# Rotary embedding on one core: four slots for x, and GpSimd products over eight positions

## The chip, the core and the metric

The kernel runs on one of the eight NeuronCores of a Trainium2 chip. A core has five engines that run their own instruction streams: TensorE (PE; its weight loads are shown apart as PEld), VectorE (DVE), ScalarE (ACT), GpSimd (POOL) and SyncE (SP). They work on SBUF, an on-chip memory of 128 partitions, and PSUM, a smaller one that TensorE writes and that GpSimd does not use here. Sixteen DMA engines move data between SBUF and the chip's main memory (HBM); transfers are issued from a queue of SP (q1 in the profile) or of ACT (q10).

The metric is the device time of one launch in microseconds (us), the median of several runs. Next to it stands one profiled execution, from which all rows are taken.

## The reference

x has the shape 8 x 2048 x 8 x 64 in float32 (batch, position, head, width): 33.55 MB in, and as much out. cos and sin are 2048 x 32.

```python
def reference(x, cos, sin):
    x1 = x[..., : x.shape[-1] // 2]
    x2 = x[..., x.shape[-1] // 2 :]
    cos = cos[None, :, None, :]
    sin = sin[None, :, None, :]
    out1 = x1 * cos - x2 * sin
    out2 = x1 * sin + x2 * cos
    return np.concatenate([out1, out2], axis=-1)
```

So every element of the output is one product with cos and one product with sin of the other half of its head, added.

## The kernel before

**Tiling.** A batch is spread over the 128 partitions with 16 positions on each; a position has 8 x 64 = 512 elements (HD), so a partition holds 8192 elements, 32 KB, of a batch. A batch is worked off in pieces, mostly of four positions (UNIT, 2048 elements); the first and the last batch have some pieces of two (lines 170 to 175).

**Buffers.** x lies in a pool of NBUF slots of 32 KB (line 45). The result overwrites x in its slot and is stored from there, so a slot is free for another batch only when the batch's stores have landed. The sin products lie in a pool `t2p` of three buffers (line 46), the cos products in one PSUM tile (`t1p`) or in a pool of two SBUF tiles (`t1s`).

**A piece** (`rotate`, line 102) is of one of three kinds:

- A, the usual one: GpSimd makes the two sin products of the halves (line 122: two instructions, each over half of the elements, one with sin and one with -sin) into a `t2` tile; VectorE makes the cos product (line 129) into PSUM and adds the two into x (line 136).
- B, the first piece of batches 2, 4 and 5: the products as in A, but the cos product goes to SBUF, and TensorE adds the two with identity matrices into PSUM (lines 143 and 144), from where ScalarE copies the sum into x (line 145).
- C, the first piece of batches 1 and 3: VectorE makes both products (lines 129 and 148), TensorE adds (lines 160 and 161), ScalarE copies (line 165). GpSimd has nothing to do.

**Order.** Each engine runs its instructions in the order of the program: `keep` holds them to it. The loop at the end goes over the batches, and in each over the pieces. Loads are issued by SP: the first NBUF batches ahead of the loop (the first batch in three parts, with the tables cos and sin after the first of them), and batch b + NBUF at the end of batch b (line 193), where it waits for b's stores. Stores are issued by ACT, one for each whole batch; the first batch is stored in three parts, and the last batch in three parts by SP (line 74).

Of the kernel before, what the change touches and what calls it, by code (L numbers as in the profile page):

```python
# [9 lines left out]
@with_exitstack  # L10
def kernel(
    ctx: ExitStack,
    tc: tile.TileContext,
    x: bass.AP,
    cos: bass.AP,
    sin: bass.AP,
    out: bass.AP,
):
    nc = tc.nc
    keep = tc.keep_in_program_order  # L20
    f32 = mybir.dt.float32
    PSUM = bass.MemoryType.PSUM

    B, S, H, D = x.shape
    Dh = D // 2
    P = 128
    HD = H * D
    R = S // P
    ROW = R * HD
    UNIT = 4 * HD  # L30
    NBUF = 5
    C = 512
    last = B - 1

    xv = x.rearrange("b (q r) h d -> b q (r h d)", q=P)
    ov = out.rearrange("b (q r) h d -> b q (r h d)", q=P)
    cos_src = cos.rearrange("(q r) d -> q r d", q=P)
    sin_src = sin.rearrange("(q r) d -> q r d", q=P)

    const_pool = ctx.enter_context(tc.tile_pool(name="const", bufs=1))  # L40
    tab_pool = ctx.enter_context(tc.tile_pool(name="tab", bufs=1, space=PSUM))
    t1_pool = ctx.enter_context(tc.tile_pool(name="t1p", bufs=1, space=PSUM))
    o_pool = ctx.enter_context(tc.tile_pool(name="op", bufs=1, space=PSUM))
    t1s_pool = ctx.enter_context(tc.tile_pool(name="t1s", bufs=2))
    xpool = ctx.enter_context(tc.tile_pool(name="xpool", bufs=NBUF))
    t2_pool = ctx.enter_context(tc.tile_pool(name="t2p", bufs=3))

    cos_sb = const_pool.tile([P, R, Dh], f32, tag="cb")
    sin_sb = const_pool.tile([P, R, Dh], f32, tag="sb")
    nsin = const_pool.tile([P, R, Dh], f32, tag="ns")  # L50
    eye = const_pool.tile([P, P], f32, tag="eye")
    neye = const_pool.tile([P, P], f32, tag="neye")
    cos_ps = tab_pool.tile([P, R, Dh], f32, tag="cp")
    sin_ps = tab_pool.tile([P, R, Dh], f32, tag="sp")

    xts = {}

    def spans(sizes):
        lo = 0
        for n in sizes:  # L60
            yield lo, n
            lo += n

    def load(b):
        xt = xpool.tile([P, ROW], f32, tag="xt", name=f"xt{b}")
        for lo, n in spans([UNIT, UNIT, 2 * UNIT] if b == 0 else [ROW]):
            keep(nc.sync.dma_start(out=xt[:, lo : lo + n], in_=xv[b, :, lo : lo + n]))  # L67
            if b == 0 and lo == 0:
                keep(nc.sync.dma_start(out=cos_sb, in_=cos_src))  # L69
                keep(nc.sync.dma_start(out=sin_sb, in_=sin_src))  # L70
        xts[b] = xt

    def store(b, lo, n):
        queue = nc.sync if b == last else nc.scalar
        keep(queue.dma_start(out=ov[b, :, lo : lo + n], in_=xts[b][:, lo : lo + n]))  # L75

    for b in range(NBUF):
        load(b)

    nc.gpsimd.memset(eye, 0.0)  # L80
    nc.gpsimd.affine_select(
        out=eye,
        in_=eye,
        compare_op=mybir.AluOpType.not_equal,
        fill=1.0,
        base=0,
        pattern=[[-1, P]],
        channel_multiplier=1,
    )
    keep(nc.scalar.mul(nsin, sin_sb, -1.0))  # L90
    keep(nc.scalar.copy(sin_ps, sin_sb))  # L91
    keep(nc.scalar.mul(neye, eye, -1.0))
    keep(nc.vector.tensor_copy(cos_ps, cos_sb))  # L93

    def rep(a, n):
        return dataclasses.replace(a, ap=[a.ap[0][:], a.ap[1][:], [0, n], a.ap[-1][:]])

    kinds = {}
    for b, kind in ((1, "C"), (2, "B"), (3, "C"), (4, "B"), (5, "B")):
        kinds[(b, 0)] = kind  # L100

    def rotate(b, lo, n):
        kind = kinds.get((b, lo), "A")
        xt = xts[b][:, lo : lo + n]
        r0 = lo // HD
        nr = n // HD
        xk = xt.rearrange("p (r k d) -> p r k d", r=nr, d=Dh)
        xu = xt.rearrange("p (g u d) -> p g u d", u=2, d=Dh)
        if kind == "A":
            t1 = t1_pool.tile([P, n], f32, tag="t1")  # L110
        else:
            t1 = t1s_pool.tile([P, n], f32, tag="t1s")
        if kind == "C":
            t2 = t1s_pool.tile([P, n], f32, tag="t1s")
        else:
            t2 = t2_pool.tile([P, n], f32, tag="t2")
        t1u = t1.rearrange("p (g u d) -> p g u d", u=2, d=Dh)
        t2u = t2.rearrange("p (g u d) -> p g u d", u=2, d=Dh)
        if kind != "C":
            for u, tab in ((1, sin_sb), (0, nsin)):  # L120
                keep(
                    nc.gpsimd.tensor_mul(  # L122
                        out=t2u[:, :, u, :].rearrange("p (r h) d -> p r h d", h=H),
                        in0=xu[:, :, 1 - u, :].rearrange("p (r h) d -> p r h d", h=H),
                        in1=rep(tab[:, r0 : r0 + nr, :], H),
                    )
                )
        keep(
            nc.vector.tensor_mul(  # L129
                out=t1.rearrange("p (r k d) -> p r k d", r=nr, d=Dh),  # L130
                in0=xk,
                in1=rep(cos_ps[:, r0 : r0 + nr, :], 2 * H),
            )
        )
        if kind == "A":
            keep(nc.vector.tensor_add(out=xt, in0=t1, in1=t2))  # L136
        elif kind == "B":
            for j in range(n // (2 * C)):
                o = o_pool.tile([P, 2 * C], f32, tag="o")
                for k in range(2):  # L140
                    cs = slice((2 * j + k) * C, (2 * j + k + 1) * C)
                    oc = o[:, k * C : (k + 1) * C]
                    nc.tensor.matmul(oc, eye, t1[:, cs], start=True, stop=False)  # L143
                    nc.tensor.matmul(oc, eye, t2[:, cs], start=False, stop=True)  # L144
                keep(nc.scalar.copy(xt[:, 2 * j * C : 2 * (j + 1) * C], o))  # L145
        else:
            keep(
                nc.vector.tensor_mul(  # L148
                    out=t2.rearrange("p (r k d) -> p r k d", r=nr, d=Dh),
                    in0=xk,  # L150
                    in1=rep(sin_ps[:, r0 : r0 + nr, :], 2 * H),
                )
            )
            G = C // Dh
            for u in range(2):
                o = o_pool.tile([P, n // 2], f32, tag="o")
                for j in range(n // 2 // C):
                    oc = o[:, j * C : (j + 1) * C]
                    gs = slice(j * G, (j + 1) * G)
                    nc.tensor.matmul(oc, eye, t1u[:, gs, u, :], start=True, stop=False)  # L160
                    nc.tensor.matmul(  # L161
                        oc, eye if u else neye, t2u[:, gs, 1 - u, :], start=False, stop=True
                    )
                keep(
                    nc.scalar.copy(  # L165
                        xu[:, :, u, :], o.rearrange("p (g d) -> p g d", d=Dh)
                    )
                )

    def pieces(b):  # L170
        if b == 0:
            return [2 * HD, 2 * HD, UNIT, UNIT, UNIT]
        if b == last:
            return [UNIT, UNIT, UNIT, 2 * HD, 2 * HD]
        return [UNIT] * 4

    def shares(b):
        if b == 0:
            return [HD, 7 * HD, 2 * UNIT]
        if b == last:  # L180
            return [2 * UNIT, UNIT, UNIT]
        return [ROW]

    for b in range(B):
        done = 0
        outs = list(spans(shares(b)))
        for lo, n in spans(pieces(b)):
            rotate(b, lo, n)
            done = lo + n
            while outs and sum(outs[0]) <= done:  # L190
                store(b, *outs.pop(0))
        if b + NBUF <= last:
            load(b + NBUF)

# [29 lines left out]
```

## Time and profile before

| | before |
|---|---|
| median of 3 runs | 163.81 us (163.28 to 164.0) |
| span of the profiled execution | 161.6 us |
| data moved by DMA | 67.65 MB, a mean of 419 GB/s over the span |
| VectorE, last add ends | 153.4 us |
| last store issued | 153.4 us, landed 7.3 us later |
| 4 MB loads of x, issue to landing | median 39.0 us |
| 4 MB stores, issue to landing | median 28.3 us |

The page of a profile gives for each engine the busy time, its share of the span and the number of instructions; then the span in 40 equal slices with a digit for the busy share of each slice in tenths (9 is 90% or more), for the DMA engines too. The groups of instructions name line, engine, operation, output and inputs with their shapes, the number of instructions; then the busy time and the mean duration in ns; then the idle time of the engine just ahead of them with what ended it. The order of time has the start in us, the duration in us, the engine, the line, and in brackets the idle time of the engine ahead of it with its releaser. The DMA view of a stretch gives the packets and bytes that each queue moved in it, and their share of the 16 engines' time. Releasers and waits are inferred by the profiler from semaphores.

### The profile page before, as it was taken

The page shows a single profiled execution, that of the slowest core. Times are in us where ns is not written, and L with a number is a line of the kernel's source. Part 1 is how long each engine was busy: PE and PEld are TensorE (multiplying, and loading weights), DVE is VectorE, ACT ScalarE, POOL GpSimd, SP SyncE. Part 2 cuts the span into 40 slices and gives each one's busy share as a digit, 9 for nine tenths or more (in the row PEclk, how much of TensorE's full clock was granted, in tenths as well). Part 3 has the DMA queues.
Part 4 walks back from the last instruction along what each step waited for, and adds up shares of the span by engine and source line. Part 5 has one row for each costly group of instructions (what it writes and reads, how often), then busy time and mean ns, then how long its engine had stood idle before and what let it go on. Part 6 is the DMA issues. An engine that isn't in the chain of part 4 may idle for free.

```text
span 161.6 us, 460 instructions
## 1 busy us (share of the span) xinstructions
PE 47.2 (29%) x80; PEld 17.8 (11%) x80; DVE 140.1 (87%) x66; ACT 12.8 (8%) x14; POOL 139.0 (86%) x70
## 2 busy tenths in 40 slices
PE   0000000497208760878029752972000000000000
PEld 0000000133003210222014211330000000000000
DVE  0468899999999999999999999999899998999900
ACT  3200000002200220021000220022000000000000
POOL 1299999999999899999996999998999969999200
PEclk9999999999965997599855998799555555555555
DMA  5999998899999999999999999999999999999995
GB/s 183 414 442 467 424 472 373 373 430 503 398 389 454 454 454 389 471 438 389 471 438 389 454 456 389 446 454 398 446 448 406 446 446 406 446 446 430 385 414 215
DMA packets 3458, 67.65 MB, mean 419 GB/s; under 512 B 384, under 2 KB 384, under 8 KB 768
## 3 DMA queue, kind: packets, MB, share of 16 engines
q1 hardware_dynamic: 2160, 38.27, 55.8%
q10 hardware_dynamic: 1296, 29.36, 42.2%
q14 instruction: 2, 0.02, 0.0%
HBM read 34.08 MB, written 33.55 MB: 419 GB/s over the span
## 4 chain that ended last, share of the span: by engine, by line
DMA 46%; DVE 37%; POOL 9%; issue 2%; SPq 1%; DVEq 0%; POOLq 0%; ACTq 0%
DMA xt<-in_x_dram 24%; DVE t L129 18%; DMA out_dram<-xt 18%; DVE xt L136 17%; POOL t L122 9%; DMA sin_sb<-in_sin_dram 3%; DVE t L148 1%; SPq L69 0%; SPq L67 0%; DVEq L136 0%; POOLq L122 0%; ACTq L75 0%
## 5 line engine op out<-in xcount | busy, mean ns | idle before, releaser
L122 POOL TENSOR_TENSOR t<-xt,sin_sb 128x1024 f32<-128x1024 f32 (+1 forms) x32 | 70.5, 2204 | 10.8 <-DMA sin_sb<-in_sin_dram 5.8
L129 DVE TENSOR_TENSOR t<-xt,cos_ps 128x2048 f32<-128x2048 f32 (+1 forms) x34 | 73.4, 2166 | 0.8
L122 POOL TENSOR_TENSOR t<-xt,nsin 128x1024 f32<-128x1024 f32 (+1 forms) x32 | 70.5, 2203 | 0.0
L136 DVE TENSOR_TENSOR xt<-t,t 128x2048 f32<-128x2048 f32 (+1 forms) x29 | 62.2, 2144 | 6.1 <-POOL t L122 3.7
L143 PE MATMUL o<-t,eye 128*128 128x512 f32 x24 | 16.5, 778 | 23.7 <-DVE t L129 20.2
L160 PE MATMUL o<-t,eye 128*128 128x512 f32 x16 | 10.6, 749 | 39.1 <-DVE t L129 36.9
L144 PE MATMUL o<-t,eye 128*128 128x512 f32 x24 | 14.7, 701 | 0.0
L145 ACT COPY xt<-o 128x1024 f32<-128x1024 f32 x6 | 6.1, 1012 | 45.7 <-PE o L144 45.7
L143 PEld LDWEIGHTS o<-t,eye 128*128 128x128 f32 x24 | 5.3, 244 | 32.8 <-issue 26.8
L160 PEld LDWEIGHTS o<-t,eye 128*128 128x128 f32 x16 | 3.6, 247 | 44.5 <-POOL t L122 30.6
L165 ACT COPY xt<-o 128x1024 f32<-128x1024 f32 x4 | 4.0, 1012 | 47.1 <-PE o L161 47.1
L144 PEld LDWEIGHTS o<-t,eye 128*128 128x128 f32 x24 | 5.7, 239 | 8.0 <-issue 8.0
L93 DVE COPY cos_ps<-cos_sb 128x512 f32<-128x512 f32 x1 | 0.7, 695 | 6.3 <-DMA cos_sb<-in_cos_dram 6.3
L161 PE MATMUL o<-t,neye 128*128 128x512 f32 x8 | 6.0, 847 | 0.2 <-DVE t L148 0.2
L148 DVE TENSOR_TENSOR t<-xt,sin_ps 128x2048 f32<-128x2048 f32 x2 | 4.6, 2279 | 0.0
L161 PE MATMUL o<-t,eye 128*128 128x512 f32 x8 | 4.1, 592 | 0.0
L161 PEld LDWEIGHTS o<-t,neye 128*128 128x128 f32 x8 | 1.8, 251 | 4.3 <-issue 2.7
L161 PEld LDWEIGHTS o<-t,eye 128*128 128x128 f32 x8 | 1.5, 190 | 1.9 <-issue 1.9
L90 ACT ACT_TABLE_LOAD x1 | 1.3, 1283 | 0.7 <-PEq L208 0.7
L90 ACT ACTIVATE nsin<-sin_sb 128x512 f32<-128x512 f32 x1 | 0.6, 630 | 5.0 <-DMA sin_sb<-in_sin_dram 5.0
L91 ACT COPY sin_ps<-sin_sb 128x512 f32<-128x512 f32 x1 | 0.6, 579 | 0.0
L80 POOL MEMSET eye<- 128x128 f32 x1 | 0.2, 205 | 0.3 <-POOLq L208 0.3
(6 smaller groups left out, 1.0 us busy)
## 6 DMA issues: line engine op xcount, KB each, us to landing
xt<-in_x_dram SPq DMA_DIRECT2D x7, 4096.0 KB, 39.0
out_dram<-xt ACTq DMA_DIRECT2D x6, 4096.0 KB, 28.3
xt<-in_x_dram SPq DMA_DIRECT2D x2, 1024.0 KB, 6.1
xt<-in_x_dram SPq DMA_DIRECT2D x1, 2048.0 KB, 11.5
out_dram<-xt ACTq DMA_DIRECT2D x1, 2048.0 KB, 25.3
out_dram<-xt SPq DMA_DIRECT2D x1, 2048.0 KB, 12.3
out_dram<-xt SPq DMA_DIRECT2D x2, 1024.0 KB, 8.7
out_dram<-xt ACTq DMA_DIRECT2D x1, 1792.0 KB, 20.2
```

The lines of the kernel that those rows point to most:

```text
L90: keep(nc.scalar.mul(nsin, sin_sb, -1.0))
L93: keep(nc.vector.tensor_copy(cos_ps, cos_sb))
L122: nc.gpsimd.tensor_mul(out=t2u[:, :, u, :].rearrange("p (r h) d -> p r h d", h=H), in0=xu[:, :, 1 - u, :].rearrange("p (r h) d -> p r h d" ...
L129: nc.vector.tensor_mul(out=t1.rearrange("p (r k d) -> p r k d", r=nr, d=Dh), in0=xk, in1=rep(cos_ps[:, r0 : r0 + nr, :], 2 * H),)
L136: keep(nc.vector.tensor_add(out=xt, in0=t1, in1=t2))
L143: nc.tensor.matmul(oc, eye, t1[:, cs], start=True, stop=False)
L144: nc.tensor.matmul(oc, eye, t2[:, cs], start=False, stop=True)
L145: keep(nc.scalar.copy(xt[:, 2 * j * C : 2 * (j + 1) * C], o))
L148: nc.vector.tensor_mul(out=t2.rearrange("p (r k d) -> p r k d", r=nr, d=Dh), in0=xk, in1=rep(sin_ps[:, r0 : r0 + nr, :], 2 * H),)
L160: nc.tensor.matmul(oc, eye, t1u[:, gs, u, :], start=True, stop=False)
L161: nc.tensor.matmul(oc, eye if u else neye, t2u[:, gs, 1 - u, :], start=False, stop=True)
L165: nc.scalar.copy(xu[:, :, u, :], o.rearrange("p (g d) -> p g d", d=Dh))
```

## The change

The number of slots for x goes from five to four. The sin products are taken out of `rotate` into a new function `cross`, which makes them for a span of its own, named by a new function `wides`. In batch 0 the spans are 2, 2, 4 and 8 positions; in batches 1 and 3, whose first piece needs none, 4 and 8; in batches 2 and 4, 8 and 8; in batches 5 and 6, 4, 4 and 8; in batch 7 they are the pieces themselves, as before. `rotate` takes the part that it needs out of the wide tile. The pool `t2p` still has three buffers, which are now of 16 KB instead of 8 KB on each partition. The pieces, kinds, cos products, adds and stores stay as they are.

```diff
-    NBUF = 5
+    NBUF = 4
...
+    t2s = {}
+
+    def cross(b, lo, n):
+        xt = xts[b][:, lo : lo + n]
+        r0 = lo // HD
+        nr = n // HD
+        xu = xt.rearrange("p (g u d) -> p g u d", u=2, d=Dh)
+        t2 = t2_pool.tile([P, n], f32, tag="t2")
+        t2u = t2.rearrange("p (g u d) -> p g u d", u=2, d=Dh)
+        for u, tab in ((1, sin_sb), (0, nsin)):
+            keep(
+                nc.gpsimd.tensor_mul(
+                    out=t2u[:, :, u, :].rearrange("p (r h) d -> p r h d", h=H),
+                    in0=xu[:, :, 1 - u, :].rearrange("p (r h) d -> p r h d", h=H),
+                    in1=rep(tab[:, r0 : r0 + nr, :], H),
+                )
+            )
+        t2s[b] = (t2, lo, n)
+
     def rotate(b, lo, n):
...
         if kind == "C":
             t2 = t1s_pool.tile([P, n], f32, tag="t1s")
         else:
-            t2 = t2_pool.tile([P, n], f32, tag="t2")
+            wide, wlo, wn = t2s[b]
+            t2 = wide[:, lo - wlo : lo - wlo + n]
         t1u = t1.rearrange("p (g u d) -> p g u d", u=2, d=Dh)
         t2u = t2.rearrange("p (g u d) -> p g u d", u=2, d=Dh)
-        if kind != "C":
-            for u, tab in ((1, sin_sb), (0, nsin)):
-                keep(
-                    nc.gpsimd.tensor_mul(
...
-                    )
-                )
...
+    def wides(b):
+        if b == 0:
+            return [(0, 2 * HD), (2 * HD, 2 * HD), (UNIT, UNIT), (2 * UNIT, 2 * UNIT)]
+        if b == last:
+            return list(spans(pieces(b)))
+        if (b, 0) in kinds and kinds[(b, 0)] == "C":
+            return [(UNIT, UNIT), (2 * UNIT, 2 * UNIT)]
+        if b >= 5:
+            return [(0, UNIT), (UNIT, UNIT), (2 * UNIT, 2 * UNIT)]
+        return [(0, 2 * UNIT), (2 * UNIT, 2 * UNIT)]
...
+        ahead = wides(b)
         for lo, n in spans(pieces(b)):
+            if ahead and ahead[0][0] == lo:
+                cross(b, *ahead.pop(0))
             rotate(b, lo, n)
```

More of the change, by code (lines that the diff above doesn't have):

```diff
@@ L115, in rotate @@
         else:
-            t2 = t2_pool.tile([P, n], f32, tag="t2")
+            wide, wlo, wn = t2s[b]
+            t2 = wide[:, lo - wlo : lo - wlo + n]
         t1u = t1.rearrange("p (g u d) -> p g u d", u=2, d=Dh)
         t2u = t2.rearrange("p (g u d) -> p g u d", u=2, d=Dh)
-        if kind != "C":
-            for u, tab in ((1, sin_sb), (0, nsin)):
-                keep(
[L122 to L125, printed above, removed]
-                    )
-                )
         keep(
```

## The prediction

> **What bounds the kernel now.** I read the page first, then the groups kept apart by shape, then the order of time on VectorE and GpSimd, and last the DMA queues in three stretches. The page:
>
> ```profile
> span 161.6 us, 460 instructions
> PE 47.2 (29%) x80; PEld 17.8 (11%) x80; DVE 140.1 (87%) x66; ACT 12.8 (8%) x14; POOL 139.0 (86%) x70
> ...
> DVE  0468899999999999999999999999899998999900
> ACT  3200000002200220021000220022000000000000
> POOL 1299999999999899999996999998999969999200
> ...
> DMA  5999998899999999999999999999999999999995
> ```
>
> Three resources are full at once: VectorE, GpSimd and the 16 DMA engines. The DMA engines move 67.65 MB and are full from the first microseconds to the last, so little can be gained here; but VectorE is also never idle, so a pause of VectorE moves its end one for one. In the order of time its last add ends at 153.40, and the last store, issued at 153.44, takes 7.3 us to land (160.7), because other stores are ahead of it. The 1 MB alone needs less: its packets took 3.3 us (157.1 to 160.4 in the packet records) and 0.4 to be counted; with the 1.0 us from issue to first packet of the first load, 4.7. So VectorE may end about 2.6 us later for nothing, and not more.
>
> ```profile
> L129 DVE TENSOR_TENSOR t<-xt,cos_ps 128x2048 f32<-128x2048 f32 x30 | 68.5, 2291 | 0.7
> L122 POOL TENSOR_TENSOR t<-xt,sin_sb 128x1024 f32<-128x1024 f32 x28 | 65.5, 2338 | 5.0 <-DMA xt<-in_x_dram 2.7 <-DVE xt L136 1.9
> L122 POOL TENSOR_TENSOR t<-xt,sin_sb 128x512 f32<-128x512 f32 x4 | 5.1, 1267 | 5.8 <-DMA sin_sb<-in_sin_dram 5.8
> ```
>
> **What larger GpSimd products save.** In the order of time the 1024-element products start 2.28 us apart and the 512-element ones 1.21: 1.07 for 512 elements and 0.14 that is fixed. A 2048-element one is in no row; I take 0.14 + 4 x 1.07 = 4.42, bounded by 4.28 (nothing fixed) and 4.56 (nothing saved). The change turns 64 products into 46: 18 x 0.14 = 2.5 us of GpSimd time less. That is all it removes. Work, bytes, VectorE's and TensorE's instructions and the order of every queue stay, except that load 4 moves behind the stores of batch 0.
>
> The Trainium skill ("Perfetto Trace Analysis", Optimizing Scalar/DVE Operations) says that grouping into larger operations can help where an engine is saturated, and that breaking up can let work finish sooner where it is not. GpSimd at 86% would come under the first half, and by it the sum would be up to 2.5 us faster, 161.3; the rows below say the opposite, and I go by them.
>
> **What it costs: batch 0.** A wide pair writes both halves only with its second product, so the add of its first four positions waits for all eight.
>
> ```profile
> 16.51 2.33 POOL L122 TENSOR_TENSOR t<-xt,sin_sb 128x1024 f32<-128x1024 f32 x1
> 18.79 2.33 POOL L122 TENSOR_TENSOR t<-xt,nsin 128x1024 f32<-128x1024 f32 x1
> 18.92 2.30 DVE L129 TENSOR_TENSOR t<-xt,cos_ps 128x2048 f32<-128x2048 f32 x1
> 21.32 2.29 DVE L136 TENSOR_TENSOR xt<-t,t 128x2048 f32<-128x2048 f32 x1
> ```
>
> Today the pair that starts at 16.51 is done at 21.12, and the add goes at 21.32. The wide pair, with the same start, is done at 16.51 + 8.84 + 0.05 = 25.40, so the add is 4.1 us late. Behind it on VectorE stands everything else; batch 0 ends at 32.4 instead of 28.3. Its store is not late (it is queued behind others until 39.4 in the packet records).
>
> Batches 1 to 3 keep the 4.1 us and add none: in batch 1 the wide pair is done at 38.8 for an add at 39.77 + 4.1 = 43.9; in batch 2 at 48.1 and 56.9 for 55.4 and 60.1; in batch 3 it waits for its buffer until batch 2's last add ends (63.0 + 4.1 = 67.1) and is done at 76.1 for 78.6. Batch 4: x arrives at 73.0, the pairs run 76.1 to 84.9 to 93.8, the adds want them at 90.1 and 94.8. It ends at 97.7 + 4.1 = 101.8.
>
> **Batches 5 and 6, the turn of the buffers.** There are three buffers for GpSimd's results before and after, but now a buffer is held until the second of two adds. The program as built shows who gets which. The buffer of batch 5's second tile was last read by batch 4's last add; that of batch 6's second tile by batch 5's last add. So GpSimd, until now some 10 us ahead, is held to the batch boundary, and then makes 4 and 8 positions in a row while VectorE consumes:
>
> - Batch 5: second tile 101.9 to 106.5, its add at 106.5. Wide pair 106.5 to 115.4; at 4.72 us a piece (18.92 to 23.64 above) the third add is due at 111.3: 4.1 us of waiting. End 122.4 instead of 114.2.
> - Batch 6: second tile 122.5 to 127.1 (its add is due at 129.6, in time), wide pair 127.2 to 136.1, third add due at 134.3: 1.8 us. End 143.1 instead of 133.4.
> - Batch 7 is not widened; its first add no longer waits (0.72 today, of which 0.6 comes back). From first to last add's end 16.9 us as today: 145.55 + 16.9 = 162.5 instead of 153.4.
>
> **Four slots.** Load 4 is issued when the stores of batch 0 have landed. Today load 5 waits for just that and goes at 53.7, but load 4 is still ahead of it, so nothing is lost. Loads and stores share the engines packet by packet:
>
> ```profile
> DMA packets 288, 8.39 MB, mean 442 GB/s; under 512 B 32, under 2 KB 32, under 8 KB 32
> ## 3 DMA queue, kind: packets, MB, share of 16 engines
> q10 hardware_dynamic: 144, 4.19, 51.2%
> q1 hardware_dynamic: 144, 4.19, 51.1%
> ```
>
> That is 54 to 73 us, load 4 (q1) beside store 1 (q10). After the change q1 is empty when load 3 ends (52.5), and load 4 comes in late. How late: the 2 MB store of batch 7 is issued on q1 at 143.53, and from 133 to 147.6 the trace has packets of q10 alone:
>
> ```profile
> DMA packets 209, 6.32 MB, mean 433 GB/s; under 512 B 16, under 2 KB 16, under 8 KB 16
> ## 3 DMA queue, kind: packets, MB, share of 16 engines
> q10 hardware_dynamic: 209, 6.32, 100.3%
> ```
>
> So a queue joining a busy engine needs some 4.2 us (first packet 147.7); the first load, on idle engines, took 1.0. I take 4.2: load 4 starts at 57.9 instead of 52.7, 5.2 us late. The 433 GB/s of one queue alone are as good as the 442 of two, so no bandwidth is lost; the stores run ahead by that much, and from load 5 on the slot is free before the queue is empty. Each later load is 5 us late: batch 4's x at 78.2 instead of 73.0, so its second wide pair ends at 95.95 for an add at 94.8: 1.1 us more. Batches 5 to 7 arrive at 97.4, 117, 136.4, before GpSimd's turn in the sum above (101.9 for the second tile, 115.3, 136). Bounds: 0 (entry in 1.0 us, or stores starved so that the load catches up), and 2.7 (load 4 keeps step with a late store 1, so the gap comes at load 5 instead: some 7 us late, and batch 5's pair slips by that much).
>
> The Trainium skill ("DMA: Bandwidth & Descriptors", Latency and other measured facts) gives about 0.6 us to the first byte of such a queue. The row is seven times that on a busy engine; by the page the load would be 1.8 us late and cost nothing, and the sum would be some 170.
>
> **The sum.** The DMA engines run dry near 141 (store 5), since store 6 is issued only at 143.2; it runs from 144.2 to 153.9, the 2 MB of batch 7, issued at 152.7, start between 153.9 and 156.9 and need 4.85, the next 1 MB 2.4: 161.2 to 164.2. The last store is issued at 162.5 and lands after 4.7 us at 167.2, or, if the queue holds it, 167.9; today 160.7: +6.5 to +7.2. With 0 to 1.1 for the slots I take +7.2. The profiled execution has a span of 161.6, and the median of the runs is 163.81, 2.2 more for what lies around it; that stays. 163.81 + 7.2 = **171.0 us**.
>
> **Rivals.**
> - Only the slots cost. If the buffers turn differently than I read, or GpSimd's lead covers the pairs, what is left is x arriving 5 us late. For it: GpSimd waits for x at batches 4, 6 and 7 today (0.78, 0.72, 1.22), so nothing hides a late load there. Batch 7 ends 21.7 us after x lands (131.7 to 153.4): 136.7 + 21.7 = 158.4, + 4.7 = 163.1, +2.4: 166.2 us. Against it: batch 0's 4.1 needs no buffer at all.
> - No change, 163.8 us. One mechanism: VectorE's delay stays below the 2.6 us that the last store can give, since the saved 2.5 us and 48 KB of buffers instead of 24 let GpSimd run further ahead in batches 4 to 6. It decides if GpSimd's lead there is over 4.1 us. Against: the second tiles of batches 5 and 6 can't start before a batch ends. A gain over 0.5% would need DMA engines with idle time to give, and they have about 3 us at both ends together.
> - Worse, about 176: the engines run dry a second time around 53, where store 1 is issued 4.1 us late (51.0) with store 0 ending at 53, and the load bound of 2.7 comes on top.
>
> **Chances.** Forecast 0.75, only the slots 0.09, worse 0.08, no change 0.06, a gain 0.02. Range: the terms add 6.5 - 0.8 (nothing fixed in a product, three pairs on the path at 0.28) = +5.7 at the low end, and 7.2 + 0.8 + 2.7 = +10.7 at the high end: 169.5 to 174.5. I lower the bottom to 167.5 towards the slots-only case. Half a per cent, 0.8 us, is what a measurement can tell: faster 0.02, within 0.06, slower 0.92.
>
> **What would show it.** GpSimd's wide products at 4.4 to 4.5 us; VectorE waiting some 4 us for GpSimd in batches 0 and 5 and 2 us in batch 6, each at the first add of a wide pair; GpSimd waiting for VectorE's add, not for DMA, ahead of the second tiles of batches 5 and 6; VectorE's end near 162; a dip of DMA around 141 to 144. It is wrong if VectorE's idle time stays near today's 13 us (the sum of its groups' idle), or if VectorE ends late and the span does not.

## The result

The changed kernel takes 170.53 us (median of four runs, 170.15 to 170.68) where the kernel before took 163.55 beside it (four runs): a ratio of 1.0428, 95% interval 1.0411 to 1.0444, 7.0 us slower. The forecast was 171.0. The profiled execution took 170.15, with a span of 168.3 against 161.6. Here and below, medians, ranges and ratios leave out a run that took over 1.5% longer than the fastest of the same kernel: two of experiment 1 (166.26 and 166.32) and one of experiment 8 (170.68).

The page of the changed kernel's profile, with the same rows as before the change:

```profile
span 168.3 us, 443 instructions
PE 47.5 (28%) x80; PEld 17.9 (11%) x80; DVE 140.1 (83%) x66; ACT 12.8 (8%) x14; POOL 136.3 (81%) x52
...
DVE  0477909999999999999999699963999959999980
...
POOL 1399999999999950994999787998869999998100
...
DMA  5999999999999999989999999999999993599966
```

GpSimd's busy time fell by 2.7 us (139.0 to 136.3), VectorE's stayed at 140.1, and the span grew by 6.7. In slices of 4.2 us, VectorE's row has new holes at the 6th, 23rd, 27th, 28th and 33rd, GpSimd's at the 16th (63 to 67 us), and the DMA row, full to the end before, dips at the 34th and 35th. The groups kept apart by shape show VectorE's adds before (L136), its adds now (L147) and the new product:

```profile
L136 DVE TENSOR_TENSOR xt<-t,t 128x2048 f32<-128x2048 f32 x25 | 57.3, 2291 | 4.5 <-POOL t L122 2.3
...
L147 DVE TENSOR_TENSOR xt<-t,t 128x2048 f32<-128x2048 f32 x25 | 57.3, 2291 | 14.9 <-POOL t L113 13.2 <-DVE t L140 0.4
L113 POOL TENSOR_TENSOR t<-xt,sin_sb 128x2048 f32<-128x2048 f32 x9 | 40.3, 4473 | 8.2 <-DVE xt L147 5.7 <-DMA xt<-in_x_dram 2.5
```

These adds of VectorE now wait 14.9 us in all, 4.5 before, and 13.2 of it for GpSimd, 2.3 before. In the kernel before, the adds of the third pieces of batches 4, 5 and 6 do not wait (the prediction shows that of batch 0, at 21.32); the last row is the last add (columns: start, duration, engine, line; a bracket holds the idle time ahead and its releaser):

```profile
90.70 2.29 DVE L136 TENSOR_TENSOR xt<-t,t 128x2048 f32<-128x2048 f32 x1
...
107.16 2.29 DVE L136 TENSOR_TENSOR xt<-t,t 128x2048 f32<-128x2048 f32 x1
...
126.42 2.29 DVE L136 TENSOR_TENSOR xt<-t,t 128x2048 f32<-128x2048 f32 x1
...
152.18 1.22 DVE L136 TENSOR_TENSOR xt<-t,t 128x1024 f32<-128x1024 f32 x1
```

In the changed kernel the same adds, and that of batch 0, wait:

```profile
25.28 2.29 DVE L147 TENSOR_TENSOR xt<-t,t 128x2048 f32<-128x2048 f32 x1 [4.20 <-POOL t L113]
...
95.86 2.29 DVE L147 TENSOR_TENSOR xt<-t,t 128x2048 f32<-128x2048 f32 x1 [1.59 <-POOL t L113]
...
116.49 2.29 DVE L147 TENSOR_TENSOR xt<-t,t 128x2048 f32<-128x2048 f32 x1 [4.27 <-POOL t L113]
...
137.23 2.29 DVE L147 TENSOR_TENSOR xt<-t,t 128x2048 f32<-128x2048 f32 x1 [1.92 <-POOL t L113]
...
162.41 1.23 DVE L147 TENSOR_TENSOR xt<-t,t 128x1024 f32<-128x1024 f32 x1
```

Each of the four that wait is the first add of a wide pair, in batches 0, 4, 5 and 6, and VectorE ends at 163.64 instead of 153.40. GpSimd's order of time shows what held GpSimd itself. Before, it did not wait ahead of the second tiles of batches 5 and 6:

```profile
97.80 2.32 POOL L122 TENSOR_TENSOR t<-xt,sin_sb 128x1024 f32<-128x1024 f32 x1
...
116.89 2.32 POOL L122 TENSOR_TENSOR t<-xt,sin_sb 128x1024 f32<-128x1024 f32 x1
```

Now it does (102.95 and 123.58), and elsewhere:

```profile
66.92 4.46 POOL L113 TENSOR_TENSOR t<-xt,sin_sb 128x2048 f32<-128x2048 f32 x1 [5.50 <-DVE xt L147]
...
78.04 4.47 POOL L113 TENSOR_TENSOR t<-xt,sin_sb 128x2048 f32<-128x2048 f32 x1 [2.19 <-DMA xt<-in_x_dram]
...
97.47 2.33 POOL L113 TENSOR_TENSOR t<-xt,sin_sb 128x1024 f32<-128x1024 f32 x1 [1.64 <-DMA xt<-in_x_dram]
...
102.95 2.32 POOL L113 TENSOR_TENSOR t<-xt,sin_sb 128x1024 f32<-128x1024 f32 x1 [0.87 <-DVE xt L147]
...
123.58 2.32 POOL L113 TENSOR_TENSOR t<-xt,sin_sb 128x1024 f32<-128x1024 f32 x1 [1.99 <-DVE xt L147]
```

At 66.9, 102.95 and 123.6 it waited for a buffer (an add of VectorE had to end), at 78.0 and 97.5 for a late x. The DMA engines, in stretches near the end (columns: stretch, length, busy time of PE, PEld, DVE, ACT, POOL with instruction counts, clock, DMA share, GB/s):

```profile
112.00:134.00 22.00, 3.70 (x8) 1.44 (x8) 17.26 (x9) 1.78 (x2) 19.33 (x8) 0.71 1.00 432
134.00:141.00 7.00, 0.00 (x0) 0.00 (x0) 5.05 (x3) 0.00 (x0) 7.00 (x3) 0.50 0.90 389
141.00:146.00 5.00, 0.00 (x0) 0.00 (x0) 4.93 (x3) 0.00 (x0) 5.00 (x3) 0.50 0.25 105
```

Between 141 and 146 they stand still for three quarters of the time: store 5 is out, store 6 is issued only at 144.2.

### The profile page after: what moved, and what is told of

It is laid out like the page before. It is cut to its first block, busy times and chain, and to the rows that moved or that the text cites. A ratio compares the mean times of both kernels' runs of the same rounds, so it can differ in the third digit from the quotient of the medians.

```text
span 168.3 us, 443 instructions
## 1 busy us (share of the span) xinstructions
PE 47.5 (28%) x80; PEld 17.9 (11%) x80; DVE 140.1 (83%) x66; ACT 12.8 (8%) x14; POOL 136.3 (81%) x52
## 2 busy tenths in 40 slices
DMA packets 3458, 67.65 MB, mean 402 GB/s; under 512 B 384, under 2 KB 384, under 8 KB 768
## 4 chain that ended last, share of the span: by engine, by line
POOL 33%; DVE 30%; DMA 30%; issue 2%; SPq 1%; DVEq 0%; POOLq 0%
POOL t L113 33%; DVE xt L147 18%; DMA xt<-in_x_dram 14%; DMA out_dram<-xt 13%; DVE t L140 12%; DMA sin_sb<-in_sin_dram 3%; SPq L67 0%; SPq L69 0%; DVEq L147 0%; POOLq L113 0%
## 5 line engine op out<-in xcount | busy, mean ns | idle before, releaser
L113 POOL TENSOR_TENSOR t<-xt,sin_sb 128x1024 f32<-128x1024 f32 (+2 forms) x23 | 68.5, 2980 | 19.4 <-DVE xt L147 9.0
L147 DVE TENSOR_TENSOR xt<-t,t 128x2048 f32<-128x2048 f32 (+1 forms) x29 | 62.2, 2144 | 16.5 <-POOL t L113 14.5
L113 POOL TENSOR_TENSOR t<-xt,nsin 128x1024 f32<-128x1024 f32 (+2 forms) x23 | 68.7, 2986 | 0.0
```

The source lines that it names most:

```text
L113: nc.gpsimd.tensor_mul(out=t2u[:, :, u, :].rearrange("p (r h) d -> p r h d", h=H), in0=xu[:, :, 1 - u, :].rearrange("p (r h) d -> p r h d" ...
```

## The experiments

Ten kernels were run, each beside the kernel before on the same chip. Besides the time, the end of VectorE in the profile is given, because it tells the theories apart where the time is blurred by the last stores. The profile is of one of the runs, not of the median one.

**1. Four slots alone.** The kernel before with one line changed.

```diff
-    NBUF = 5
+    NBUF = 4
```

> The kernel before with four slots and nothing else: GpSimd's products stay at four positions, with three buffers of 8 KB. Theory (slots and wide products act together): load 4 enters the queue 5 us late, each later x arrives 4 to 5 us late, VectorE waits for GpSimd's first products of batches 5 to 7; batch 7's x lands near 136.5, VectorE ends 21.7 us later at 158.2, and the time is 165.2 to 166.4. Rival A (the slots cost nothing, all 7 us of the change are the wide products): 163.6. Rival B (the slots are the whole cost): 170.5.

Measured: 164.09 (eight runs, 163.27 to 165.64), ratio 1.0039 (1.0002 to 1.0077). The profile is of the run of 163.27; x of batch 7 landed at 135.1 instead of 131.7, and VectorE ended at 156.8 instead of 153.4. So the late x is there, and it costs something in some runs and nothing in others, the profiled one among these: 0.6 us by the ratio, less than the theory said and far from the 7.0. VectorE's longest wait in it is the second piece's add of batch 5:

```profile
105.98 2.29 DVE L136 TENSOR_TENSOR xt<-t,t 128x2048 f32<-128x2048 f32 x1 [3.59 <-POOL t L122]
```

**2. Batch 0 without wide products.** The changed kernel, edited in `wides`:

```diff
         if b == 0:
-            return [(0, 2 * HD), (2 * HD, 2 * HD), (UNIT, UNIT), (2 * UNIT, 2 * UNIT)]
+            return list(spans(pieces(b)))
```

> The changed kernel with batch 0's products at two and four positions as before, all else as changed. Theory: VectorE's wait of 4.2 us in batch 0 goes, batches 0 to 3 end 4 us earlier, but batch 4's x still lands near 78, its second wide pair still ends near 95.8, so the wait comes back there (about 4 us longer at that add than the 1.6 of the changed kernel) and nothing is gained: 170.0 to 170.9. Rival (waits of VectorE add up, as my prediction summed them): 166.4.

Measured: 170.44 (170.30 to 170.60), ratio 1.0431 (1.0416 to 1.0447), VectorE's end 163.9. Nothing was gained. The wait did not vanish, it moved, for the most part to batch 4 (VectorE, order of time):

```profile
96.07 2.29 DVE L147 TENSOR_TENSOR xt<-t,t 128x2048 f32<-128x2048 f32 x1 [4.30 <-POOL t L113]
```

1.59 us in the changed kernel, 4.30 here, at nearly the same moment (and 1.17 in batch 2): batch 4's x lands at 78.1, GpSimd then makes its two wide pairs one behind the other until 96.0, and nothing that VectorE gains earlier survives that. With four slots, batch 0's 4.2 us are covered by the late load and these pairs.

**3. Batches 5 and 6 without wide products.** The changed kernel:

```diff
         if b >= 5:
-            return [(0, UNIT), (UNIT, UNIT), (2 * UNIT, 2 * UNIT)]
+            return list(spans(pieces(b)))
```

> The changed kernel with batches 5 and 6 at four positions, batches 0 to 4 wide as changed. Theory: VectorE's waits of 4.3 and 1.9 us at the wide pairs of batches 5 and 6 go; what is left is x arriving late, VectorE ends near 158.2 and the time is 165.3 to 166.3, the same as with four slots alone. Rival (the waits of batch 0 and 4 are kept besides the slots' cost): 168 or more.

Measured: 164.88 (164.33 to 165.41), ratio 1.009 (1.0063 to 1.0117), VectorE's end 158.1. Batches 0 to 4 are still wide, with waits of 4.2 and 1.9 us, and the ratio lies between those of the two kernels here that have four slots and no wide product (1.0039 in run 1, 1.0131 in run 7). The wide products of batches 5 and 6 make up some 5.5 of the 7.0 us (1.0428 against 1.009).

**4. One more buffer for the second tiles of batches 5 and 6.** The changed kernel with a pool of one 8 KB buffer:

```diff
+    t2x_pool = ctx.enter_context(tc.tile_pool(name="t2x", bufs=1))
...
-        t2 = t2_pool.tile([P, n], f32, tag="t2")
+        extra = b in (5, 6) and lo == UNIT
+        t2 = (t2x_pool if extra else t2_pool).tile([P, n], f32, tag="t2x" if extra else "t2")
```

> The changed kernel with one more buffer of 8 KB, which only the second tile of batches 5 and 6 gets, so that it doesn't wait for the batch before to end. Theory (in batch 5 the late x holds GpSimd nearly as long as the buffer did, 0.9 us apart; in batch 6 the buffer holds it 2.2 us): the third add of batch 5 0.9 us earlier, VectorE's end 2.2 us earlier, 168.0 to 169.0. Rival (the turn of the buffers is the whole of both waits, as my prediction had it): 4 to 6 us less, 164.5 to 166.5.

Measured: 168.31 (168.16 to 168.91), ratio 1.0312 (1.0291 to 1.0334), VectorE's end 161.65, 2.0 us earlier. The waits at the two wide pairs:

```profile
115.96 2.29 DVE L149 TENSOR_TENSOR xt<-t,t 128x2048 f32<-128x2048 f32 x1 [3.50 <-POOL t L115]
...
135.24 2.29 DVE L149 TENSOR_TENSOR xt<-t,t 128x2048 f32<-128x2048 f32 x1 [0.46 <-POOL t L115]
```

4.27 became 3.50 and 1.92 became 0.46. So the buffers hold GpSimd for some 2 us of VectorE's time. The rest is x that lands late and the wide pair's own length: from batch 5's first product, which waits for x until 97.83, GpSimd runs without a pause to the end of the pair, and so it does in batch 6 from 117.17.

**5. Eight half slots, wide products.** The four slots are cut into eight of 16 KB, each loaded and stored by itself, so that the load queue does not run empty.

```diff
-    xpool = ctx.enter_context(tc.tile_pool(name="xpool", bufs=NBUF))
+    xpool = ctx.enter_context(tc.tile_pool(name="xpool", bufs=2 * NBUF))
...
-        xt = xpool.tile([P, ROW], f32, tag="xt", name=f"xt{b}")
-        for lo, n in spans([UNIT, UNIT, 2 * UNIT] if b == 0 else [ROW]):
-            keep(nc.sync.dma_start(out=xt[:, lo : lo + n], in_=xv[b, :, lo : lo + n]))
+        xts[b] = []
+        for lo, n in spans([UNIT, UNIT, 2 * UNIT] if b == 0 else [HALF, HALF]):
+            if lo in (0, HALF):
+                xts[b].append(xpool.tile([P, HALF], f32, tag="xt", name=f"xt{b}_{lo}"))
+            keep(nc.sync.dma_start(out=part(b, lo, n), in_=xv[b, :, lo : lo + n]))
...
```

> The changed kernel with its four slots cut into eight halves of 16 KB: each half is loaded and stored by itself, so load 4's first half only waits for the first two stores of batch 0 (landed at 39) and the load queue doesn't run empty. The wide products and their three buffers stay. Theory (the wide products and the turn of their three buffers are enough by themselves, the late x adds about 1 us): x of batches 4 to 7 lands near 73, 92, 112 and 132 as before the change, VectorE still waits some 4 us in batch 0 and some 4 us at the wide pair of batch 5 and ends near 162.5, time 168.6 to 169.8. Rival (without late x GpSimd's lead covers the wide pairs): VectorE ends at 157 or earlier, 163.5 to 165.5.

Measured: 165.72 (165.19 to 166.36), ratio 1.0141 (1.0111 to 1.0171), VectorE's end 159.5: between the two theories. VectorE waits 4.20 us in batch 0, 1.20 in batch 5 and 1.73 in batch 6. The edit changed more than it should: in this build batch 5's second tile gets a buffer that waits for TensorE in batch 4, not for batch 4's last add, so GpSimd starts it at 99.0 instead of 102.95; and a half slot brings the first half of a batch earlier, while the second halves of batches 4 to 7 landed at 77.8, 97.3, 116.8 and 136.2, as late as whole batches in the changed kernel. The run does not separate the causes; run 9 was made for that.

**6. Eight half slots, products of four positions, six buffers of 8 KB.** The kernel before with the half slots of run 5 and `bufs=6` for `t2p`.

> The kernel before with the same 128 KB for x as eight halves of 16 KB, and the freed memory for six instead of three buffers of 8 KB for GpSimd's products of four positions. Theory (the DMA engines bound the kernel before; four slots only cost through the empty load queue): x lands as with five slots, VectorE ends at 153.4 or earlier, and the time is that of before, 163.1 to 163.8. Rival (fewer bytes of x in memory cost in any case): 164.5 or more.

Measured: 164.44 (164.37 to 164.56), ratio 1.0062 (1.0047 to 1.0077): neither. VectorE ends at 152.8, earlier than in any other kernel, never waits for GpSimd after batch 0, and the time is 1.0 us longer. The last store, issued at 152.82, took 8.8 us to land, so here the DMA engines set the time. They are full throughout. Two stretches of the kernel before:

```profile
30.00:45.00 15.00, 9.63 (x16) 3.49 (x16) 14.62 (x8) 2.02 (x2) 15.00 (x8) 1.00 0.97 418
60.00:100.00 40.00, 19.69 (x32) 7.31 (x32) 39.14 (x19) 4.22 (x5) 37.46 (x17) 0.79 1.01 434
```

and of this one:

```profile
30.00:45.00 15.00, 10.44 (x16) 3.75 (x16) 14.62 (x8) 2.02 (x2) 15.00 (x8) 1.00 1.02 435
60.00:100.00 40.00, 19.62 (x32) 7.31 (x32) 38.75 (x18) 4.96 (x5) 39.18 (x18) 0.80 1.01 430
```

435 GB/s for 418 in the one and 430 for 434 in the other (5330 packets for the same 67.65 MB, 3458 before). Up to 16 packets of 32 KB, 0.5 MB, straddle each end of a stretch, so 1% of 40 us, 0.2 MB, cannot be read from it; over the 100 us from 30 to 130 it is 432 for 431. So no loss of steady rate is shown, and where the 1.0 us goes stays open.

**7. Four slots, products of four positions, six buffers of 8 KB.** The kernel before with `NBUF = 4` and `bufs=6` for `t2p`, the memory of the changed kernel.

> The kernel before with four slots of 32 KB and six buffers of 8 KB for GpSimd's products of four positions (the memory of the changed kernel, without wide products). Theory (late x, not the buffers, makes VectorE wait with four slots): as with four slots and three buffers, 164 to 165.6. Rival (the deeper lead of GpSimd hides the late x): 163.5.

Measured: 165.34 (164.82 to 166.06), ratio 1.0131 (1.0100 to 1.0162), VectorE's end 158.3. More buffers do not hide a late x: batch 4's landed at 78.6 here and at 76.5 in the profile of run 1, and by the ratio this kernel is slower than run 1's. Why x came later is not shown. GpSimd's longest wait says what the buffers are worth: it now runs ahead until x is missing.

```profile
78.71 2.33 POOL L122 TENSOR_TENSOR t<-xt,sin_sb 128x1024 f32<-128x1024 f32 x1 [7.46 <-DMA xt<-in_x_dram]
```

**8. Five slots, the wait of a wide pair in batch 0 alone.** The kernel before, products of four positions in their 8 KB buffers, but the four products of batch 0's last two pieces in the order that makes the first add wait for all of them.

```diff
...
+        t2 = t2_pool.tile([P, n], f32, tag="t2")
+        product(b, lo, n, t2, 1)
+        if (b, lo) in ((0, 2 * UNIT),):
+            nxt = t2_pool.tile([P, n], f32, tag="t2")
+            product(b, lo + n, n, nxt, 1)
+            product(b, lo + n, n, nxt, 0)
+            early[(b, lo + n)] = nxt
+        product(b, lo, n, t2, 0)
...
```

> The kernel before, five slots and products of four positions, but in batch 0 GpSimd makes the four products of the last two pieces in the order sin of the one, sin of the next, -sin of the next, -sin of the one, so that the first of the two adds has to wait for all of them, as with a wide pair. Theory (a wait of VectorE is carried to its end when x is on time, but the first 3.3 us at the end are free, because the last store stands behind others): the add waits 4.3 us, the waits of 0.3, 0.5 and 0.7 us later on go, VectorE ends near 156.2 instead of 153.4, and the time is unchanged, 163.2 to 163.9. Rival (every wait of VectorE is paid): 166 or more.

Measured: 165.28 (four runs, 164.43 to 165.85), ratio 1.0108 (1.0069 to 1.0147), and VectorE's end 157.0. The add of batch 0 waited 4.50:

```profile
25.76 2.29 DVE L155 TENSOR_TENSOR xt<-t,t 128x2048 f32<-128x2048 f32 x1 [4.50 <-POOL t L110]
```

The wait was carried to the end, 0.8 us further than expected, since smaller waits of 0.33, 0.20 and 0.20 stayed, and the time was not unchanged. The profile is of the run of 164.43: VectorE ended 3.6 us later than before, and the run took 1.1 more. That is past the 3.3 us that the expectation called free, so it does not refute them.

**9. The same order in batches 0, 5 and 6, still with five slots.**

```diff
-        if (b, lo) in ((0, 2 * UNIT),):
+        if (b, lo) in ((0, 2 * UNIT), (5, 2 * UNIT), (6, 2 * UNIT)):
```

> As the run with batch 0's paired order, and the same order for the last two pieces of batches 5 and 6: the waits of the wide products without wide tiles, without four slots and without late x. Theory (the waits themselves, not the late x, are the main cost of the change; and buffers that come free only at the end of a batch hold GpSimd back): x of batches 4 to 7 lands as before at 73, 92, 112 and 132; VectorE waits 4.3 us in batch 0, 4.6 in batch 5 and about 2 in batch 6 and ends near 163; 168.3 to 170.5. Rival (late x is needed for the cost): 165 or less.

Measured: 170.06 (169.99 to 170.67), ratio 1.0418 (1.0388 to 1.0448), VectorE's end 163.5. x of batch 4 landed at 71.7, of batch 7 at 131.8. VectorE's order of time:

```profile
25.65 2.29 DVE L155 TENSOR_TENSOR xt<-t,t 128x2048 f32<-128x2048 f32 x1 [4.49 <-POOL t L110]
...
116.03 2.29 DVE L155 TENSOR_TENSOR xt<-t,t 128x2048 f32<-128x2048 f32 x1 [4.70 <-POOL t L110]
...
137.07 2.29 DVE L155 TENSOR_TENSOR xt<-t,t 128x2048 f32<-128x2048 f32 x1 [2.22 <-POOL t L110]
```

With five slots, x on time and no wide tile, such waits alone cost as much as the change does: 170.06 against 170.53.

**10. Half of the wait in batch 0.** As run 8, with the order of the last three products changed.

```diff
             product(b, lo + n, n, nxt, 1)
+            product(b, lo, n, t2, 0)
             product(b, lo + n, n, nxt, 0)
             early[(b, lo + n)] = nxt
+            return t2
         product(b, lo, n, t2, 0)
```

> As the run with batch 0's paired order at five slots, but the first piece's second product comes third of the four, not last, so that its add waits some 2.2 us instead of 4.5. Theory (VectorE has some free time at its end; the run with 4.5 us of waiting ended VectorE at 157.0 and was just over it): VectorE ends near 154.9 and the time is unchanged, 163.2 to 163.9. Rival (there is no free time, the waits of VectorE are paid from the first): about half of that run's 2.4 us, 164.4 or more.

Measured: 163.33 (eleven runs, 163.29 to 163.94), ratio 0.9996 (0.9986 to 1.0006). The add waited 2.22 us:

```profile
23.45 2.29 DVE L157 TENSOR_TENSOR xt<-t,t 128x2048 f32<-128x2048 f32 x1 [2.22 <-POOL t L110]
```

VectorE ended at 154.8, and the time is the same. There is free time at the end: a VectorE that ends 1.4 us later costs nothing, one that ends 3.6 later cost 1.1 in the profiled run of experiment 8 (1.8 by the ratio of its four runs).

No version here beats the kernel before. The one with the earliest end of VectorE (run 6) is slower, since its last store has to wait for the DMA engines.

## Why the prediction held, and where its steps were off

**The size of the product.** 4.42 us was taken for 2048 elements; they start 4.41 to 4.45 apart.

**The waits.** 4.1 us was worked out for batch 0 (4.20), 1.1 for batch 4 (1.59), 4.1 for batch 5 (4.27) and 1.8 for batch 6 (1.92). Run 3 shows those of batches 5 and 6 to be the main cost, and run 9 that waits of this size in batches 0, 5 and 6 are enough without the slots and without a wide tile.

**Four slots.** Load 4 was to enter at 57.9; its first packet came at 57.78, 4.06 us after its issue at 53.73. From 54 to 57.5 the queue of the stores ran alone at full rate in the changed kernel:

```profile
DMA packets 48, 1.57 MB, mean 449 GB/s; under 512 B 0, under 2 KB 0, under 8 KB 0
## 3 DMA queue, kind: packets, MB, share of 16 engines
q10 hardware_dynamic: 48, 1.57, 104.0%
```

No bandwidth was lost there, as worked out, and the x of batches 4 to 7 landed at 77.9, 97.3, 116.8 and 136.4 (78.2, 97.4, 117 and 136.4 in the sum). The Trainium skill ("DMA: Bandwidth & Descriptors", Latency and other measured facts) gives about 0.6 us to the first byte; on engines busy with another queue this run has 4.06, and the measurement decides. (As an estimate from that page's 0.6 us the load would have been 1.6 us late, 53.7 + 0.6 against 52.7, not the 1.8 that the prediction has.) The entry does not always take 4 us: batch 7's first store had its first packet after 2.62 us in run 8 and after 1.06 in the changed kernel, where store 6 was nearly out.

**What adding hides.** The sum carried batch 0's 4.1 us to the end and put the slots on top at 0 to 1.1. As one chain of waits it held: 162.5 and 1.1 make 163.6 for VectorE's end, which came at 163.64. But its terms are not what each part is worth. Run 2 shows that with four slots batch 0's wait is worth nothing, because the late x of batch 4 and batch 4's own wide pairs stop VectorE anyway: 4.30 us instead of 1.59. With x on time it is carried (run 8: 3.6 us at VectorE's end). The two causes cover each other, so the total comes out the same whichever is counted.

**The turn of the buffers.** It was named as the cause of both late waits. It holds GpSimd 0.87 us in batch 5 and 1.99 in batch 6, and run 4 gives it some 2 us of the time. In batch 5 the late x (97.3) and two products ahead of the pair reach to 102.1 by themselves, 0.9 before the buffer was free. With x on time the buffers take that place: in run 9 GpSimd never waits for x, but 2.18 us for an add at 92.6, and batch 5's pair makes VectorE wait 4.70.

**The end.** The sum gave the last store 4.7 us from issue to landing when nothing is ahead of it. That was too much: issued at 163.66 it landed at 167.50, 3.84 later, and it took 3.84 or 3.85 in runs 1 to 5, 7 and 9 too. Before, it took 7.29, so VectorE's end has 3.4 us free and not 2.6. Run 1's profile shows these whole: VectorE ends 3.4 us later (156.8), and the span is 161.5 against 161.6. In run 8's, with 0.2 more, the last store needed 4.73, 0.9 more, and the run took 1.1 more. Once the free time is used up, the span ends some 4.7 us after VectorE: 156.8 and 161.5 in run 1, 158.1 and 162.8 in run 3, 161.65 and 166.4 in run 4, 163.5 and 168.2 in run 9, 163.64 and 168.3 here.

**How near it came is in part luck.** With the slots at their full 1.1 and the store at its 4.7 the sum would have been 163.6 + 4.7 = 168.3, 7.6 more than the 160.7 of before. The sum took 7.2, from the middle of its terms; measured are 6.8 us in the landing and the span and 7.0 in the time. The other half of the miss of 0.5 us is the time before, 163.81 in the forecast and 163.55 beside the changed kernel.

**The rivals.** Only the slots (166.2): run 1 has 164.1, since most of its lag falls into the free time. No change through GpSimd's lead: run 7 shows that the lead ends where x is missing. The engines running dry around 53: they move 393 GB/s from 50 to 54 where 432 is usual, some 0.4 us less, and the packets that straddle the ends make that figure rough.

## What to carry to other kernels

A larger instruction on a producer saves its fixed part (0.14 us of 2.28 here, 2.7 us in all), but its consumer then waits for the whole of it: look at the lead that the producer has at that moment, which is set by the last buffer freed and the last input landed, not by its busy share. Where two delays end at the same consumer they cover each other, so undoing one of them can gain nothing, and a sum of waits is right only along one chain. When the DMA engines are full, look for how late the compute may end for free before pricing a wait.

## What was not expected of the hardware

Cutting 4 MB transfers into halves (3458 to 5330 packets) made no difference to the steady rate of the full DMA engines that could be measured: 432 GB/s for 431 from 30 to 130 us. Even so the kernel with the halves was slower by 0.62% (0.47 to 0.77) with an earlier end of VectorE, for a reason that no run here shows.

The five kernels whose VectorE ends between 156.8 and 159.5 (runs 1, 3, 5, 7 and 8) scatter by 1.1 to 2.4 us, run 1 from 163.3 to 165.6; the others, with an earlier or a later end, by 0.2 to 0.8. With four runs of most of them this is a hint, and its cause is not shown.
